# A first tile's norm split over two engines and two load queues, and a low-rank gate projection in four column groups of the array

## The chip, the cores and the metric

The kernel runs on all 8 cores of one Trainium2 chip (two dies, cores 0 to 3 and 4 to 7). Each core handles one prompt of 2048 tokens and four sample sequences of 8 tokens. The metric is the device time of the slowest core in microseconds. The kernel before took 2364.44 us (median of 3 runs, 2363.14 to 2366.65).

Some executions fall into a slower state, in which the cores of one die have a lower granted TensorE clock (in the trace of the kernel before, die 1 had 0.897 and 2576.0 us, die 0 had 0.993 and 2355.7 us).

- An *undisturbed die* is a die of one execution on which all four cores have a granted clock above 0.985.
- Each such die gives the mean of its four spans. I average these over all executions of a kernel and subtract the same average for the kernel before, run in the same series. The result is quoted with its standard error.

This measure is not the metric (in the fast runs of the kernel before the slowest core is 6 to 13 us above the mean of the cores). It uses more of the data and compares like with like.

## The reference, cut to what matters

```python
# D_MODEL 1024; GLA: 4 heads, DK 128, DV 256, gate rank 16
x = x + 0.5 * swiglu_ffn(rmsnorm(x, g[0]), w_in, w_out)       # first thing that any tile does: a norm of x
h = rmsnorm(x, g[1])
q, k, v, g_lr, r = split(h @ w_in)                            # g_lr has 16 columns
log_a = log_sigmoid(g_lr @ w_g2 + b_g) / 16                   # 16 -> 512: the second gate matrix
# for every chunk of the recurrence (the sample sequences have one chunk of 8 tokens):
o = attn @ v  +  (q * exp(cum)) @ state                       # inside the chunk + from the old state
# ... output norm, output gate, w_out; second half-FFN; shared K/V; a second layer with window attention
```

## The kernel before

Activations are transposed: 1024 features lie as 8 chunks of 128 partitions, with tokens along the free axis. Each core has four prompt tiles (t0 to t3, 512 tokens each) and one sample tile (32 tokens). Tiles are written as Python generators. A scheduler of the kernel's own runs them when the kernel is *built* and fixes the instruction order of every engine, from an estimated cost of each operation.

```python
def c_mm(count, n):                     # estimated cost of matmuls, us
    return count * max(n / 2400.0 + 0.0026, 0.0265)

# Threads.run: the operation that could start first by the estimates, ties within 0.15 us by urgency
cands = [(S.start_of(th[3][1], th[3][3], th[3][4]), th) for th in self.live if th[3] is not None]
...
m = min(c[0] for c in cands) + self.TIE
th = min((c for c in cands if c[0] <= m), key=lambda c: self.urgency(c[1]))[1]
```

The load of x and the squares of the norm. ScalarE (ACT) squares eight chunks, VectorE (DVE) adds them up one after the other, and one TensorE (PE) matmul with a matrix of ones sums the partitions.

```python
def load_x(T, prev):
    nq = 4 if T.n == 512 else 1
    for q in range(nq):
        ...
        yield O(SP, (lambda e, q=q, w=w, src=src, ms=ms: e.dma_start(out=..., in_=src[:, q * w:(q + 1) * w])), ...)
    for m in range(8):
        yield from square(T, m)           # ACT square into T.h[m]; DVE add to a running sum

def norm_stats(T):
    ...
    ms = [T.sum] if n == 512 else range(8)
    yield mm(PS[b][:, 0:n], [(ones, T.h[:, m, :]) for m in ms], ...)
    ...                                   # Ln and Exp on ACT; then DVE makes h = x * gain * rs
```

The gate of the recurrence: eight matmuls with a 128x16 stationary (the operand `lhsT`; the trace shows its load as an LDWEIGHTS of 90 ns beside each matmul), then per head one matmul with a 16x128 stationary.

```python
yield from mmh(T, (PS[b][0:16, :],), lambda kt, z: WLR[:, kt, :], ["WLR"], (b,), n)
...
yield copy(ACT, glr, PS[b][0:16, :], n, [("ps", b)], [gk])
...
yield mm(PS[b], [(WG2[0:16, hd * 128:(hd + 1) * 128], glr)], [gk, "WG2"], b, n)
```

The sample tile's recurrent output, four times (one sequence each). Two matmuls of 8 columns alternate, the first with 32 rows and the second with 128:

```python
for hd in range(4):
    for f in range(2):
        e.matmul(po[:, hd * 2 + f, :], lhsT=vv[...], rhs=am[:, hd, c8], start=True, stop=False)         # 32 rows
        ins = e.matmul(po[:, hd * 2 + f, :], lhsT=S0b[...], rhs=qT[:, hd, c8], start=False, stop=True)  # 128 rows
```

The softmax here doesn't subtract the row's maximum and nothing guards it: scores larger than these inputs give would overflow.

Of the kernel before, what the change touches and what calls it, by code (L numbers as in the profile page):

```python
# [227 lines left out]
def need(cond):  # L228
    return ("need", cond)
# [80 lines left out]
def build():  # L310
    nc = bass.Bass("TRN2", target_bir_lowering=False)

    def din(name, shape):
        return nc.dram_tensor(name, list(shape), F32, kind="ExternalInput").ap()
# [4 lines left out]
    xp = din("xp", [4, 128, 4096]); xs = din("xs", [128, 256]); st_in = din("st", [16, 128, 256])  # L319
    ck = din("ck", [4, 128, 3328]); cv = din("cv", [4, 128, 3328])  # L320
    wfi = din("wfi", [4 * NF, 128, 2048]); wfo = din("wfo", [32, 128, 2688])
    wgl = din("wgl", [16, 128, 2048]); wlr = din("wlr", [128, 128]); gg2 = din("gg2", [16, 512])
    wkv = din("wkv", [2, 128, 2048]); wqd = din("wqd", [3, 128, 2048]); wod = din("wod", [4, 128, 1536])
    cbd = din("cbd", [128, B_END - 128]); cfd = din("cfd", [128, A_END])
    rpd = din("rpd", [4, 2, 128, 512]); rsd = din("rsd", [128, 64])
# [10 lines left out]
    CB = A("CB", [128, B_END], BF16)  # L336
    CF = A("CF", [128, A_END], F32)
    SM = A("SM", [128, 8], F32)
    WLR = A("WLR", [128, 8, 16], BF16)
    WG2 = A("WG2", [16, 512], BF16)  # L340
    U = A("U", [128, 4, 256], F32)
    Sbf = A("Sbf", [128, 4, 256], BF16)
    KT = A("KT", [128, 2, 2048], BF16)
# [232 lines left out]
    def xk(T, m):  # L576
        return ("x", T.b, m)

    def hk(T, m):
        return ("h", T.b, m)  # L580

    def rk(T, what):
        return ("R", T.b, what)
# [56 lines left out]
# [3 lines that stand above are left out]
            ms = range(q * 8 // nq, (q + 1) * 8 // nq)  # L643
            if prev is not None:
                yield need(lambda: all(("y", prev.nm, m) in done for m in ms))
            if T.t == 1:
                after = units[(0, "fi0", 3 + 2 * q)]
                yield need(lambda: after.ready)
            w = len(ms) * T.n
            src = xp[T.t] if T.n == 512 else xs  # L650
            yield O(SP, (lambda e, q=q, w=w, src=src, ms=ms: e.dma_start(
                out=T.x[:, ms[0]:ms[-1] + 1, :].rearrange("p m n -> p (m n)"), in_=src[:, q * w:(q + 1) * w])),
                [after.key] if T.t == 1 else [], writes=[xk(T, m) for m in ms], cost=0.1, dma="x%s_%d" % (T.b, q), nbytes=w * 512)
        for m in range(8):
            yield from square(T, m)

# [22 lines left out]
    def norm_stats(T):  # L679

        n = T.n
        sqn = T.sqn
        yield need(lambda: all(("sq", T.nm, sqn, m) in done for m in range(8)))
        (b,) = yield from get_banks(1)
        ms = [T.sum] if n == 512 else range(8)
        yield mm(PS[b][:, 0:n], [(ones, T.h[:, m, :]) for m in ms], [hk(T, m) for m in ms] + ["ONE"], b, n)
        (i,) = yield from T.pool.get("rs", 1, 1)
        rs = T.pool.aps[i]
        k = T.pool.key(i)
        yield act(rs, PS[b][:, 0:n], AF.Ln, n, [("ps", b)], [k], bias=EPS)  # L690
        put(b)
        yield act(rs, rs, AF.Exp, n, [k], [k], scale=-0.5)
        T.sqn += 1
        return i
# [105 lines left out]
    def gla(T):  # L800
# [2 lines left out]
        h8 = hks(T)  # L803
        pool = T.pool
        (b,) = yield from get_banks(1)
        yield from mmh(T, (PS[b][0:16, :],), lambda kt, z: WLR[:, kt, :], ["WLR"], (b,), n)
        (gi,) = yield from pool.get("glr", 1, 1)
        glr, gk = pool.aps[gi][0:16, 0:256].bitcast(BF16), pool.key(gi)
        yield copy(ACT, glr, PS[b][0:16, :], n, [("ps", b)], [gk])
        put(b)  # L810
        gates = {}

        def gate():
            for hd in range(4):
                i, k_ = yield from pool.get("gate", 2, 6)
                a, c = pool.aps[i], pool.aps[k_]
                ka, kc = pool.key(i), pool.key(k_)
                (b,) = yield from get_banks(1)
                yield mm(PS[b], [(WG2[0:16, hd * 128:(hd + 1) * 128], glr)], [gk, "WG2"], b, n)
                yield act(a, PS[b], AF.Exp, n, [("ps", b), "negb"], [ka], scale=-1.0, bias=negb[:, hd:hd + 1])  # L820
                put(b)
                yield act(a, a, AF.Ln, n, [ka], [ka], bias=1.0)
                yield O(DVE, lambda e: e.tensor_tensor_scan(out=c, data0=CB[:, B_SC:B_SC + 512], data1=a, initial=0.0, op0=ALU.mult, op1=ALU.add),  # L823
                        [ka, "CB"], [kc], c_dve(1000))
                yield act(a, c, AF.Exp, n, [kc], [ka], scale=-1.0 / 16)
                yield act(c, c, AF.Exp, n, [kc], [kc], scale=1.0 / 16)
                yield copy(DVE, T.dec[:, hd, :], a[:, 127::128], 4, [ka], [("dec", T.b, hd)])
                gates[hd] = (i, k_)
            pool.put("glr", gi)
# [177 lines left out]
    def gla_s(T):  # L1007
# [19 lines left out]
        pk_ = [T.pool.key(i) for i in ids]  # L1027
        EQ, EK = A4, C4
        (b,) = yield from get_banks(1)
        yield from mmh(T, (PS[b][0:16, 0:n],), lambda kt, z: WLR[:, kt, :], ["WLR"], (b,), n)  # L1030
        glr = KB[0:16, 896:928]
        yield copy(ACT, glr, PS[b][0:16, 0:n], n, [("ps", b)], [gk])
        put(b)
# [57 lines left out]
        yield tt(am, pa, CB[0:32, B_MS:B_MS + 32].unsqueeze(1).to_broadcast([32, 4, 32]), ALU.mult, 128, [("ps", b), "CB"], [gk])  # L1091
        put(b)
        gv = [rk(T, ("gv", hd)) for hd in range(4)]
        for s in range(4):
            c8 = slice(s * 8, s * 8 + 8)
            us, ub = (yield from use(T, "S0", s)), (yield from use(T, "S0b", s))
            S0 = us.ap.bitcast(F32).rearrange("p (h w) -> p h w", h=4)
            S0b = ub.ap.rearrange("p (h w) -> p h w", h=4)
            yield copy(ACT, S0b, S0, 1024, [us.key], [ub.key])
            (b,) = yield from get_banks(1)  # L1100
            po = PS[b][:, 0:64].rearrange("p (m n) -> p m n", m=8)

            def fo(e, c8=c8, po=po, S0b=S0b):
                ins = None
                for hd in range(4):
                    for f in range(2):
                        e.matmul(po[:, hd * 2 + f, :], lhsT=vv[:, hd * 256 + f * 128:hd * 256 + (f + 1) * 128], rhs=am[:, hd, c8], start=True, stop=False)
                        ins = e.matmul(po[:, hd * 2 + f, :], lhsT=S0b[:, hd, f * 128:(f + 1) * 128], rhs=qT[:, hd, c8], start=False, stop=True)
                return ins
            yield O(PE, fo, [gk, ub.key] + gv, [("ps", b)], 1.68)  # L1110
            yield copy(ACT, oT[:, :, c8], po, 64, [("ps", b)], [rk(T, "go")])
            put(b)
            yield O(DVE, (lambda e, s=s: e.tensor_scalar(out=kms, in0=ktok, scalar1=CF[0:32, A_SQ + s:A_SQ + s + 1], scalar2=None, op0=ALU.mult)),
                    [gk, "CF"], [rk(T, "kms")], c_dve(512, 2))
            for hp in range(2):
                (b,) = yield from get_banks(1)
                pk = PS[b].rearrange("p (a w) -> p a w", a=2)

                def fk(e, hp=hp, pk=pk):
                    ins = None  # L1120
                    for a in range(2):
                        hd = 2 * hp + a
                        ins = e.matmul(pk[:, a, :], lhsT=kms[:, hd, :], rhs=vv[:, hd * 256:(hd + 1) * 256], start=True, stop=True)
                    return ins
                yield O(PE, fk, [rk(T, "kms")] + gv, [("ps", b)], c_mm(2, 256))
                for a in range(2):
                    hd = 2 * hp + a
                    yield stt(S0[:, hd, :], S0[:, hd, :], EQ[:, hd, s * 8 + 7:s * 8 + 8], pk[:, a, :], ALU.mult, ALU.add, 256, [("ps", b), us.key] + pk_, [us.key])
                put(b)
            yield O(SP, (lambda e, s=s, S0=S0: e.dma_start(out=sts_o[s * 4:(s + 1) * 4].rearrange("h p d -> p h d"), in_=S0)), [us.key], [],  # L1130
                    cost=0.1, dma="sts%d" % s, nbytes=524288)
            us.left -= 1
            ub.left -= 1
# [448 lines left out]
    def prologue():  # L1582

        yield need(lambda: units[(0, "fi0", 4)].ready)
        yield O(PL, lambda e: e.dma_start(out=CB[:, 128:], in_=cbd[:, :]), [], ["CB"], cost=1.0, dma="c1", nbytes=(B_END - 128) * 512)
        yield O(PL, lambda e: e.dma_start(out=WG2[:], in_=gg2[:, :]), [], ["WG2"], cost=1.0, dma="c2", nbytes=32768)
        yield O(PL, lambda e: e.dma_start(out=WLR[:].rearrange("p a b -> p (a b)"), in_=wlr[:, :]), [], ["WLR"], cost=1.0, dma="c3", nbytes=65536)
        yield O(SP, lambda e: e.dma_start(out=stabs[:], in_=rsd[:, :]), [], ["stabs"], cost=0.1, dma="c4", nbytes=32768)
        yield O(DVE, lambda e: e.tensor_scalar(out=negb, in0=G[:, 56:60], scalar1=-1.0, scalar2=None, op0=ALU.mult), ["CF"], ["negb"], 0.1)
        yield O(PL, lambda e: e.memset(U[:], 0.0), [], [("U", hd) for hd in range(4)], 2.0)  # L1590
# [17 lines left out]
def make_in_maps(inp, ncores=8):  # L1608
# [8 lines left out]
    def cols(w, k):  # L1617

        return w.reshape(k, 128, -1).transpose(1, 0, 2)
# [14 lines left out]
    for h in range(4):  # L1634
# [1 line left out]
    wgl = np.stack([w.reshape(128, 2048) for w in wg])  # L1636
    kvw, wq, wo = f(inp["kv_w"]), f(inp["attn_w_q"])[0], f(inp["attn_w_out"])[0]
    shared = {
        "wfi": f(wfi), "wfo": f(wfo), "wgl": f(wgl), "wlr": f(cols(glr, 8).reshape(128, 128)), "gg2": f(inp["gla_w_gate2"])[0],
        "wkv": f(np.stack([cols(kvw[:, i * 256:(i + 1) * 256], 8).reshape(128, 2048) for i in range(2)])),  # L1640
        "wqd": f(np.stack([cols(wq[:, i * 256:(i + 1) * 256], 8).reshape(128, 2048) for i in range(3)])),
        "wod": f(np.stack([cols(wo[:, i * 256:(i + 1) * 256], 6).reshape(128, 1536) for i in range(4)])),
# [40 lines left out]
```

## Time and profile before

| | kernel before |
|---|---|
| time, median of the first 3 runs | 2364.44 us |
| span and granted clock of core 0 in the trace | 2359.6 us, 0.993 |
| PE / DVE / ACT busy on core 0 | 98% / 52% / 50% |
| gate projection, second gate matrix, recurrent output (busy time on PE) | 8.6, 6.2, 11.4 us |

First look at the spans of the cores of the kernel before.

```profile
core 0: 2359.6 us, clock 0.993
...
core 2: 2362.8 us, clock 0.993
...
die 0 (median of its cores): 2355.7 us, clock 0.993
die 1 (median of its cores): 2576.0 us, clock 0.897
```

The page of core 0 of the kernel before: busy time by engine (PEld is TensorE's loading of weights), and the chain that ended last, by engine.

```profile
PE 2306.4 (98%) x14660; PEld 1129.2 (48%) x14660; DVE 1219.9 (52%) x2180; ACT 1172.5 (50%) x2316; POOL 317.2 (13%) x599
...
PE 94%; DMA 5%; issue 1%; ACT 0%; DVE 0%; SPq 0%; POOL 0%; POOLq 0%; ACTq 0%; DVEq 0%
```

TensorE is the bound. Work taken off it counts, unless it then waits for something else.

The groups of PE instructions that the change touches, kernel before, core 0. Columns: line, engine, operation, output and inputs, rows*columns of the stationary, shape, count, then busy time in us and the mean ns of one, then the idle time before them.

```profile
L615 PE MATMUL pst<-h,WLR 128*16 128x512 bf16 x32 | 8.6, 380 | 0.0
...
L615 PE MATMUL pst<-pb,WG 16*128 16x512 bf16 x16 | 6.2, 385 | 0.0
L1108 PE MATMUL pst<-KT,ring 128*128 128x8 bf16 x32 | 5.8, 180 | 0.0
L1107 PE MATMUL pst<-KT 32*128 32x8 bf16 x32 | 5.6, 175 | 0.0
```

The mean of one (380 ns and more) isn't what a matmul costs in a stream, where full-row matmuls of this shape start 216 ns apart (kernel before, core 0). For that cost one takes the distances of successive starts, in the timeline (start, length, engine, line, what, count). Kernel before, PE of core 0:

```profile
187.69 0.60 PE L615 MATMUL pst<-h,WLR 128*16 128x512 bf16 x2
188.22 1.90 PE L615 MATMUL pst<-h,ring 128*128 128x512 bf16 x8
190.06 0.38 PE L615 MATMUL pst<-pb,WG 16*128 16x512 bf16 x1
190.37 1.05 PE L615 MATMUL pst<-ring,h 128*128 128x256 bf16 x8
...
226.62 0.17 PE L1107 MATMUL pst<-KT 32*128 32x8 bf16 x1
226.72 0.18 PE L1108 MATMUL pst<-KT,ring 128*128 128x8 bf16 x1
...
228.30 0.38 PE L863 MATMUL pst<-CB,r 128*128 128x128 bf16 x4
```

From the second gate matrix's start to the next is 190.37 - 190.06 = 0.31 us, where a full-row matmul of 512 columns takes 0.216 from start to start. The recurrent-output block runs from 226.62 to 228.30, 1.68 us for 16 tiny matmuls.

The start of the kernel before, all engines of core 0. The last column is the idle time before, and what ended it:

```profile
1.97 2.73 SPq L651 DMA_DIRECT2D x<-xp  x4
...
9.98 1.15 ACT L620 ACTIVATE h<-x 128x512 bf16<-128x512 f32 x2 [2.87 <-DMA x<-xp]
...
17.45 0.69 DVE L628 TENSOR_TENSOR h<-pb,h 128x512 bf16<-128x512 f32 x1 [0.17 <-DVE pb L628]
...
21.06 2.08 DVE L631 SCALAR_TENSOR_TENSOR h<-x,CF,pb 128x512 bf16<-128x512 f32 x3 [0.73 <-ACT pb L620]
```

ACT gets the first quarter of x at about 10 us, the last DVE add starts at 17.45 and the first normed h at 21.06. Until then TensorE has almost nothing to do.

### The profile page before, as it was taken

Reading aid. Unit: us, or ns where it says so; the run is one execution under the profiler, and the core shown is the slowest. Engines: PE = TensorE matmul, PEld = TensorE weight load, DVE = VectorE, ACT = ScalarE, POOL = GpSimd, SP = SyncE. Lnnn points to the kernel's source line nnn. Section 1 sums busy time; section 2 is a strip of 40 time slices with the busy share of each in tenths; the row PEclk is TensorE's granted clock in tenths of the full one; section 3 lists DMA queues with packets and bytes.
Section 4 is the critical chain, followed back from the end, with each engine's and each line's share of the span. In section 5 each row is a group of like instructions: output and inputs, shape, how many; then the busy total and the mean of one; then the engine's idle time right before and its main releaser. Section 6 shows DMA issues by size and latency. Waiting matters only on the chain.

```text
span 2589.4 us, 42668 instructions; the slowest of 8 cores (2351.7 to 2589.4 us)
## 1 busy us (share of the span) xinstructions
PE 2542.9 (98%) x14660; PEld 1190.5 (46%) x14660; DVE 1223.3 (47%) x2180; ACT 1177.0 (45%) x2316; POOL 317.7 (12%) x599
## 2 busy tenths in 40 slices
PE   7999999999999999999999989999999999999999
PEld 3445444544444444455444435444544444444444
DVE  4424464445533446646543243454466335653742
ACT  5524544463443246455453124533555533753642
POOL 1111111101111111111111011011111111111110
PEclk8888888888888889999998878888999999999999
DMA  9986788778867788998897787667789989689794
GB/s 190 150 122 108 128 133 120 113 105 122 135 115 127 123 146 146 169 159 134 157 156 133 151 139 125 108 117 114 137 153 166 167 153 172 116 138 156 145 173 93
DMA packets 101362, 357.08 MB, mean 138 GB/s; under 512 B 12528, under 2 KB 17440, under 8 KB 101024
## 3 DMA queue, kind: packets, MB, share of 16 engines
q0 software_dynamic: 84032, 326.10, 77.7%
q1 hardware_dynamic: 17120, 28.25, 3.6%
q8 instruction: 122, 2.00, 0.3%
q14 instruction: 88, 0.72, 0.1%
HBM read 662.88 MB, written 15.40 MB: 262 GB/s over the span
## 4 chain that ended last, share of the span: by engine, by line
PE 96%; DMA 3%; issue 1%; ACT 0%; DVE 0%; SPq 0%; ACTq 0%; POOL 0%; POOLq 0%; DVEq 0%
PE pst L615 92%; DMA ring<-wfo 1%; DMA ring<-wfi 1%; PE pst L1410 1%; DMA ring<-ck 0%; PE pst L1349 0%; PE pst L987 0%; PE pst L970 0%; PE pst L988 0%; PE pst L1371 0%; DMA x<-xp 0%; PE pst L1433 0%; PE pst L1375 0%; PE pst L957 0%; PE pst L863 0%
## 5 line engine op out<-in xcount | busy, mean ns | idle before, releaser
L615 PE MATMUL pst<-h,ring 128*128 128x512 bf16 x6144 | 1531.1, 410 | 4.1 <-DVE h L631 3.3
L615 PEld LDWEIGHTS pst<-h,ring 128*128 128x128 bf16 x6144 | 623.5, 103 | 804.9 <-issue 471.8
L615 PE MATMUL pst<-r,ring 128*128 128x512 bf16 x3136 | 780.9, 409 | 6.4 <-DMA ring<-wfo 6.4
L620 ACT ACTIVATE pb<-pb 128x512 f32<-128x512 f32 x856 | 534.8, 629 | 64.7 <-DVE pb L823 4.4
L620 ACT ACTIVATE pb<-pst 128x512 f32<-128x512 f32 (+1 forms) x472 | 278.8, 595 | 567.6 <-PE pst L615 560.7
L628 DVE TENSOR_TENSOR pb<-pb,pst 128x512 f32<-128x512 f32 x368 | 252.2, 686 | 547.3 <-ACT pb L620 539.4
L615 PEld LDWEIGHTS pst<-r,ring 128*128 128x128 bf16 x3136 | 318.5, 103 | 415.6 <-issue 232.7
L511 POOL DMA_DIRECT2D ring<-wfi x336 | 178.0, 530 | 1224.4 <-PE pst L615 1150.7
L620 ACT ACTIVATE h<-x 128x512 bf16<-128x512 f32 x192 | 119.0, 627 | 391.3 <-DVE x L631 305.0
L628 DVE TENSOR_TENSOR r<-pb,pst 128x512 bf16<-128x512 f32 x336 | 230.6, 687 | 46.2 <-DVE pb L628 40.3
L631 DVE SCALAR_TENSOR_TENSOR x<-pst,x 128x512 f32<-128x512 f32 x128 | 88.3, 690 | 261.7 <-PE pst L615 261.4
L631 DVE SCALAR_TENSOR_TENSOR h<-x,CF,pb 128x512 bf16<-128x512 f32 x224 | 150.8, 746 | 13.4 <-ACT pb L620 12.6
L511 POOL DMA_DIRECT2D ring<-wfo x128 | 67.7, 529 | 605.5 <-PE pst L615 496.7
L628 DVE TENSOR_TENSOR pb<-pb,h 128x512 f32<-128x512 f32 x120 | 82.4, 689 | 43.7 <-ACT h L620 42.6
L615 PE MATMUL pst<-ring,h 128*128 128x256 bf16 x640 | 86.9, 302 | 0.0
L620 ACT ACTIVATE spb<-pst 128x32 f32<-128x32 f32 (+2 forms) x111 | 21.7, 198 | 125.0 <-PE pst L615 124.4
L615 PEld LDWEIGHTS pst<-ring,h 128*128 128x128 bf16 x640 | 67.4, 107 | 18.6 <-issue 5.1
L615 PEld LDWEIGHTS pst<-hsb,ring 128*128 128x128 bf16 x1536 | 53.9, 97 | 40.6 <-issue 35.4
L615 PE MATMUL pst<-hsb,ring 128*128 128x32 bf16 x1536 | 54.4, 178 | 14.1 <-DMA ring<-wfi 14.0
L511 POOL DMA_DIRECT2D ring<-wgl x64 | 33.9, 531 | 260.7 <-PE pst L615 238.9
L624 ACT COPY r<-pst 128x512 f32<-128x512 f32 (+3 forms) x104 | 51.0, 491 | 23.6 <-PE pst L1375 11.4
L628 DVE TENSOR_TENSOR x<-x,pst 128x512 f32<-128x512 f32 x64 | 43.9, 686 | 29.8 <-PE pst L615 29.7
(151 smaller groups left out, 1113.6 us busy)
## 6 DMA issues: line engine op xcount, KB each, us to landing
ring<-wfi POOLq DMA_DIRECT2D x336, 512.0 KB, 7.4
ring<-wfo POOLq DMA_DIRECT2D x128, 672.0 KB, 8.0
ring<-wgl POOLq DMA_DIRECT2D x64, 512.0 KB, 6.7
x<-xp SPq DMA_DIRECT2D x16, 512.0 KB, 9.6
y_p<-x SPq DMA_DIRECT2D x32, 256.0 KB, 7.8
ring<-wqd POOLq DMA_DIRECT2D x12, 512.0 KB, 9.7
ring<-wod POOLq DMA_DIRECT2D x16, 384.0 KB, 8.8
ring<-wkv POOLq DMA_DIRECT2D x8, 512.0 KB, 8.3
```

The source lines that it names most:

```text
L511: yield O(PL, (lambda e, u=u, dst=dst: e.dma_start(out=dst, in_=u.src)), first.get(u.uid, []), writes=[u.key], cost=1.0, dma="w%d_%d" % (s ...
L615: ins = e.matmul(out, lhsT=l, rhs=r, start=(start and i == 0), stop=(stop and i == last), skip_group_check=skip)
L620: return O(ACT, lambda e: e.activation(out=out, in_=in_, func=func, scale=scale, bias=bias), reads, writes, c_act(n))
L624: return O(ACT, lambda e: e.copy(out=out, in_=in_), reads, writes, c_act(n))
L628: return O(DVE, lambda e: e.tensor_tensor(out=out, in0=a, in1=b, op=op), reads, writes, c_dve(n, rate))
L631: return O(DVE, lambda e: e.scalar_tensor_tensor(out=out, in0=a, scalar=s, in1=b, op0=op0, op1=op1), reads, writes, c_dve(n))
L1410: ins = e.matmul(PS[bs[hp]][0:nk, rr * 64 + jj * 32:rr * 64 + jj * 32 + 32], lhsT=KT[hp * 64:hp * 64 + 64, jj, sl_(r, nk, 16)], rhs=T.QT[h ...
```

## The change

There are three parts, all meant to take time off TensorE or off the start:

1. *Start.* The first tile's squares are split between ACT and DVE, TensorE adds the eight of them with eight accumulating matmuls instead of DVE's chain of adds, and the odd quarters of x are issued from ACT's queue.
2. *Gate.* The eight gate-projection matmuls go to four groups of 32 columns of the array, which can run at once (in the trace before, the attention's 128*64 pairs start 3 to 4 ns apart). They leave four partial sums of two chunks each, on four groups of 32 partitions. The second gate matrix is stacked four times (padded to 32 rows each), so that its matmul, now with 128 rows, adds the partial sums.
3. *Recurrent output of the sample tile.* All 32-row matmuls are done in one run of 8 for the four sequences together, and the four blocks keep only their 128-row matmuls. DVE adds the two parts.

```diff
@@ load_x
-            yield O(SP, (lambda e, q=q, w=w, src=src, ms=ms: e.dma_start(
+            yield O(ACT if T.t == 0 and q % 2 else SP, (lambda e, q=q, w=w, src=src, ms=ms: e.dma_start(
...
+        if T.t == 0:
+            T.sum = None
+            for m in range(8):
+                if m % 2:
+                    yield stt(T.h[:, m, :], T.x[:, m, :], 1.0 / 1024, T.x[:, m, :], ALU.mult, ALU.mult, ...)
+                else:
+                    yield act(T.h[:, m, :], T.x[:, m, :], AF.Square, T.n, ..., scale=1.0 / 32)
+                done.add(("sq", T.nm, 0, m))
+            return
@@ norm_stats
-        ms = [T.sum] if n == 512 else range(8)
-        yield mm(PS[b][:, 0:n], [(ones, T.h[:, m, :]) for m in ms], [hk(T, m) for m in ms] + ["ONE"], b, n)
+        ms = [T.sum] if n == 512 and T.sum is not None else range(8)
+        for m in ms:
+            yield mm(PS[b][:, 0:n], [(ones, T.h[:, m, :])], [hk(T, m), "ONE"], b, n, start=(m == ms[0]), stop=(m == ms[-1]))
@@ gla
-        yield from mmh(T, (PS[b][0:16, :],), lambda kt, z: WLR[:, kt, :], ["WLR"], (b,), n)
+        hn = T.hn
+        for kt in range(8):
+            yield need(lambda: ("h", T.nm, hn, kt) in done)
+            p = slice(kt % 4 * 32, kt % 4 * 32 + 32)
+            yield O(PE, (lambda e: e.matmul(PS[b][p, :], lhsT=WLR[:, kt, :], rhs=T.h[:, kt, :], start=(kt < 4), stop=(kt >= 4))),
+                    [hk(T, kt), "WLR"], [("ps", b)], 0.06)
...
-                yield mm(PS[b], [(WG2[0:16, hd * 128:(hd + 1) * 128], glr)], [gk, "WG2"], b, n)
+                yield mm(PS[b], [(WG2[:, hd * 128:(hd + 1) * 128], glr)], [gk, "WG2"], b, n)
@@ gla_s
+        def fi(e):
+            ins = None
+            for m in range(8):
+                ins = e.matmul(PS[b][:, m * n:(m + 1) * n], lhsT=vv[:, m * 128:(m + 1) * 128], rhs=am[:, m // 2, :], start=True, stop=True)
+            return ins
+        yield O(PE, fi, [gk] + gv, [("ps", b)], c_mm(8, n))
...
-                        e.matmul(po[:, hd * 2 + f, :], lhsT=vv[...], rhs=am[:, hd, c8], start=True, stop=False)
-                        ins = e.matmul(po[:, hd * 2 + f, :], lhsT=S0b[...], rhs=qT[:, hd, c8], start=False, stop=True)
+                        ins = e.matmul(po[:, hd * 2 + f, :], lhsT=S0b[...], rhs=qT[:, hd, c8], start=True, stop=True)
...
-            yield copy(ACT, oT[:, :, c8], po, 64, [("ps", b)], [rk(T, "go")])
+            yield tt(oT[:, :, c8], oT[:, :, c8], po, ALU.add, 64, [("ps", b), rk(T, "go")], [rk(T, "go")])
... (cut: the padded and stacked gate weights, 0.29 MB more to load by the kernel's own byte counts)
```

More of the change, by code (lines that the diff above doesn't have):

```diff
@@ L321, in build @@
     wfi = din("wfi", [4 * NF, 128, 2048]); wfo = din("wfo", [32, 128, 2688])
-    wgl = din("wgl", [16, 128, 2048]); wlr = din("wlr", [128, 128]); gg2 = din("gg2", [16, 512])
+    wgl = din("wgl", [16, 128, 2048]); wlr = din("wlr", [128, 256]); gg2 = din("gg2", [128, 512])
     wkv = din("wkv", [2, 128, 2048]); wqd = din("wqd", [3, 128, 2048]); wod = din("wod", [4, 128, 1536])
@@ L338, in build @@
     SM = A("SM", [128, 8], F32)
-    WLR = A("WLR", [128, 8, 16], BF16)
-    WG2 = A("WG2", [16, 512], BF16)
+    WLR = A("WLR", [128, 8, 32], BF16)
+    WG2 = A("WG2", [128, 512], BF16)
     U = A("U", [128, 4, 256], F32)
@@ L650, in load_x @@
             src = xp[T.t] if T.n == 512 else xs
-            yield O(SP, (lambda e, q=q, w=w, src=src, ms=ms: e.dma_start(
+            yield O(ACT if T.t == 0 and q % 2 else SP, (lambda e, q=q, w=w, src=src, ms=ms: e.dma_start(
                 out=T.x[:, ms[0]:ms[-1] + 1, :].rearrange("p m n -> p (m n)"), in_=src[:, q * w:(q + 1) * w])),
                 [after.key] if T.t == 1 else [], writes=[xk(T, m) for m in ms], cost=0.1, dma="x%s_%d" % (T.b, q), nbytes=w * 512)
+        if T.t == 0:
+            T.sum = None
+            for m in range(8):
+                if m % 2:
+                    yield stt(T.h[:, m, :], T.x[:, m, :], 1.0 / 1024, T.x[:, m, :], ALU.mult, ALU.mult, T.n, [xk(T, m)], [hk(T, m)])
+                else:
+                    yield act(T.h[:, m, :], T.x[:, m, :], AF.Square, T.n, [xk(T, m)], [hk(T, m)], scale=1.0 / 32)
+                done.add(("sq", T.nm, 0, m))
+            return
         for m in range(8):
@@ L805, in gla @@
         (b,) = yield from get_banks(1)
-        yield from mmh(T, (PS[b][0:16, :],), lambda kt, z: WLR[:, kt, :], ["WLR"], (b,), n)
+        hn = T.hn
[4 more added lines that the diff above has]
+                    [hk(T, kt), "WLR"], [("ps", b)], 0.06)
         (gi,) = yield from pool.get("glr", 1, 1)
-        glr, gk = pool.aps[gi][0:16, 0:256].bitcast(BF16), pool.key(gi)
-        yield copy(ACT, glr, PS[b][0:16, :], n, [("ps", b)], [gk])
+        glr, gk = pool.aps[gi][:, 0:256].bitcast(BF16), pool.key(gi)
+        yield copy(ACT, glr, PS[b], n, [("ps", b)], [gk])
         put(b)
@@ L1029, in gla_s @@
         (b,) = yield from get_banks(1)
-        yield from mmh(T, (PS[b][0:16, 0:n],), lambda kt, z: WLR[:, kt, :], ["WLR"], (b,), n)
+        yield from mmh(T, (PS[b][0:16, 0:n],), lambda kt, z: WLR[:, kt, 0:16], ["WLR"], (b,), n)
         glr = KB[0:16, 896:928]
@@ L1093, in gla_s @@
         gv = [rk(T, ("gv", hd)) for hd in range(4)]
+        (b,) = yield from get_banks(1)
+        def fi(e):
[4 more added lines that the diff above has]
+        yield O(PE, fi, [gk] + gv, [("ps", b)], c_mm(8, n))
+        yield copy(ACT, oT.rearrange("p m n -> p (m n)"), PS[b][:, 0:8 * n], 8 * n, [("ps", b)], [rk(T, "go")])
+        put(b)
         for s in range(4):
@@ L1106, in fo @@
                     for f in range(2):
-                        e.matmul(po[:, hd * 2 + f, :], lhsT=vv[:, hd * 256 + f * 128:hd * 256 + (f + 1) * 128], rhs=am[:, hd, c8], start=True, stop=False)
-                        ins = e.matmul(po[:, hd * 2 + f, :], lhsT=S0b[:, hd, f * 128:(f + 1) * 128], rhs=qT[:, hd, c8], start=False, stop=True)
-                return ins
-            yield O(PE, fo, [gk, ub.key] + gv, [("ps", b)], 1.68)
-            yield copy(ACT, oT[:, :, c8], po, 64, [("ps", b)], [rk(T, "go")])
+                        ins = e.matmul(po[:, hd * 2 + f, :], lhsT=S0b[:, hd, f * 128:(f + 1) * 128], rhs=qT[:, hd, c8], start=True, stop=True)
+                return ins
+            yield O(PE, fo, [gk, ub.key], [("ps", b)], 0.3)
+            yield tt(oT[:, :, c8], oT[:, :, c8], po, ALU.add, 64, [("ps", b), rk(T, "go")], [rk(T, "go")])
             put(b)
@@ L1585, in prologue @@
         yield O(PL, lambda e: e.dma_start(out=CB[:, 128:], in_=cbd[:, :]), [], ["CB"], cost=1.0, dma="c1", nbytes=(B_END - 128) * 512)
-        yield O(PL, lambda e: e.dma_start(out=WG2[:], in_=gg2[:, :]), [], ["WG2"], cost=1.0, dma="c2", nbytes=32768)
-        yield O(PL, lambda e: e.dma_start(out=WLR[:].rearrange("p a b -> p (a b)"), in_=wlr[:, :]), [], ["WLR"], cost=1.0, dma="c3", nbytes=65536)
+        yield O(PL, lambda e: e.dma_start(out=WG2[:], in_=gg2[:, :]), [], ["WG2"], cost=1.0, dma="c2", nbytes=262144)
+        yield O(PL, lambda e: e.dma_start(out=WLR[:].rearrange("p a b -> p (a b)"), in_=wlr[:, :]), [], ["WLR"], cost=1.0, dma="c3", nbytes=131072)
         yield O(SP, lambda e: e.dma_start(out=stabs[:], in_=rsd[:, :]), [], ["stabs"], cost=0.1, dma="c4", nbytes=32768)
@@ L1638, in make_in_maps @@
     shared = {
-        "wfi": f(wfi), "wfo": f(wfo), "wgl": f(wgl), "wlr": f(cols(glr, 8).reshape(128, 128)), "gg2": f(inp["gla_w_gate2"])[0],
+        "wfi": f(wfi), "wfo": f(wfo), "wgl": f(wgl), "wlr": f(np.pad(cols(glr, 8), ((0, 0), (0, 0), (0, 16))).reshape(128, 256)),
+        "gg2": f(np.tile(np.pad(f(inp["gla_w_gate2"])[0], ((0, 16), (0, 0))), (4, 1))),
         "wkv": f(np.stack([cols(kvw[:, i * 256:(i + 1) * 256], 8).reshape(128, 2048) for i in range(2)])),
```

## The prediction

> **What bounds the kernel.** TensorE. The recorded run is in the slow state (one die at clock 0.897), so I read cores 0 and 2 of the undisturbed die (2359.6 and 2362.8 us, clock 0.993). The page of core 0 has PE busy 98%, DVE 52%, ACT 50%; its chain is 94% PE, 5% DMA. Successive starts in the trace are 216 ns apart for a 128x512 matmul, 25 ns for 128x32; start gaps over 0.4 us beyond that pace add up to only 37 to 52 us per core. From 20 to 150 us the DMA share is about 1.03: there both are full.
>
> **Costs, from the trace (core 0).**
> 1. Gate projection, four prompt tiles: 32 matmuls with a 128*16 stationary, 216 ns apart, one by one. In four column groups neighbours run at once: the attention's 128*64 pairs already start 3 to 4 ns apart. By the changed kernel's instruction order the 32 fall into 11 runs and 12 rounds: 20 x 216 ns = 4.3 us go. The runs' switch costs stay.
> 2. Second gate matrix, 16 matmuls with 16 rows: each costs about 93 ns extra going in (309 to 312 where 216 is normal) and 100 going out (317). [...] With 128 rows there is no switch: 16 x 0.19 = 3.1 us.
> 3. Sample tile's recurrent output: 64 matmuls of 8 columns alternate between 32 and 128 rows, 108 and 112 ns apart: 4 blocks of 1.68 us. After: 32 full-row ones at about 25 ns and one run of 8 with 32 rows (0.4 us with its switches): 1.2 us. Saves 5.5 us. The added copy and adds are off the path.
> Sum on TensorE: 12.9 us, in stages (170 to 420, 1380 to 1600 us) where it does not wait for DMA.
> 4. Start. On core 2 the last quarter of x lands at 13.7, the DVE adds end at 15.9, the sum matmul starts at 17.0, h comes from 19.4. The change should bring h about 3 us earlier; 7 extra matmuls fall into idle time. But the first weight units land at 16.5 and 20.5, DMA is at 100%, and TensorE already waits for weights at 44 to 48 us on three of four cores. An earlier start is mostly paid back there[...]. The second queue: [...] issuing four quarters took 1.9 to 2.7 us here. The first quarter, which releases the first weights, may even land later. Net: -1 us (-3 to +1).
>
> **Sum.** -13 us of TensorE time, some 80% passing through (weight waits near 540 to 600, 850 and the 8 to 10 us one at 1330 us may grow), and -1: 2364.4 - 11.5 = 2353 us. Eight times in ten between 2344 and 2362. Faster by over 2%: 0.01; within 2%: 0.98; slower: 0.01.
>
> **What would show it.** Gate projection matmuls 3 to 5 ns apart within a round; second-gate matmuls at 216 ns without jumps; recurrent-output blocks of about 0.2 us; first h before 17 us, but the first weight matmul not before 17 and more waiting for weights before 50 us; the wait near 1320 still there.
>
> **What would make it wrong.** The instruction order changes throughout the first 450 us and may add or remove waits. Four column groups might not overlap. A DMA-bound first stage could swallow the later gains, or a gain at the start could pass through whole.

80% of -13 us, and -1 for the start, come to about -11.5 us. The -1 was given as one figure, without parts, so it is my estimate. In the traces of core 0 the loads of WG and WLR grew by 144 KB together (16 to 128 and 32 to 64 KB); at the 177 GB/s that this core moved from 20 to 150 us before, that is an estimated 0.8 us.

## More of the kernel before

The verdicts on whole runs use fast runs alone.

At 82 us the sum matmul of the second prompt tile's norm (`h,CB`, CB holds the ones) stands in the timeline of the kernel before, core 0:

```profile
81.99 0.38 PE L615 MATMUL pst<-h,CB 128*128 128x512 bf16 x1
...
82.20 0.56 PE L615 MATMUL pst<-hsb,ring 128*128 128x32 bf16 x16
...
82.61 3.61 PE L615 MATMUL pst<-h,ring 128*128 128x512 bf16 x16
...
84.58 5.39 DVE L631 SCALAR_TENSOR_TENSOR h<-x,CF,pb 128x512 bf16<-128x512 f32 x8
```

While ACT and DVE turn that sum into the tile's normed h (from 84.58), TensorE has 16 matmuls of the sample tile (`hsb`) and 16 of another prompt tile to do. It does not wait. The same kernel does wait at the same kind of place later: at about 935 us TensorE stands idle for 2.9 us on all four undisturbed cores, between a norm's sum and its h.

## The result, and the profile after

The changed kernel is correct and took 2357.65 us (median of 4 runs, 2355.72 to 2358.66), beside 2363.79 us for the kernel before in the same rounds (4 runs, 2361.63 to 2366.65). That is 6.1 us less. The ratio is 0.9972, with a 95% interval of 0.9955 to 0.999. Ratios are the mean time of one kernel's fast runs over that of the other's fast runs of the same rounds, so they are not quite the ratio of the medians quoted. The time lies inside the predicted range; of the predicted gain of 11.5 us about half arrived.

The kernel after, spans of the cores. Both dies are undisturbed:

```profile
core 0: 2342.4 us, clock 0.994
core 1: 2355.6 us, clock 0.993
...
die 0 (median of its cores): 2350.4 us, clock 0.993
die 1 (median of its cores): 2349.3 us, clock 0.993
```

The same page lines of core 0 after the change:

```profile
PE 2295.2 (98%) x14643; PEld 1125.0 (48%) x14643; DVE 1218.0 (52%) x2181; ACT 1168.3 (50%) x2309; POOL 317.0 (14%) x599
...
PE 95%; DMA 3%; issue 1%; ACT 1%; DVE 0%; SPq 0%; ACTq 0%; DVEq 0%; POOLq 0%
```

PE's busy time fell by 11.2 us. (Core 0 alone fell by 17 us in span, but cores of one run differ by that much: 2338.7 to 2355.6 after. One core of one run proves nothing at this size.)

The groups that the change made, kernel after, core 0:

```profile
L615 PE MATMUL pst<-pb,WG 128*128 128x512 bf16 x16 | 6.1, 379 | 0.0
...
L822 PE MATMUL pst<-h,WLR 128*32 128x512 bf16 x32 | 5.2, 388 | 0.0
...
L1134 PE MATMUL pst<-KT,ring 128*128 128x8 bf16 x32 | 1.4, 166 | 0.0
...
L1116 PE MATMUL pst<-KT 32*128 32x32 bf16 x8 | 0.4, 173 | 0.0
```

And their timeline on PE, kernel after:

```profile
182.91 0.40 PE L822 MATMUL pst<-h,WLR 128*32 128x512 bf16 x3
...
222.73 0.34 PE L1134 MATMUL pst<-KT,ring 128*128 128x8 bf16 x8
222.93 2.32 PE L615 MATMUL pst<-h,ring 128*128 128x512 bf16 x10
```

Three gate-projection matmuls together take 0.40 us, as long as one (0.38 us for the single one at 183.23): in a run of eight, starts within a group of four were 2 to 4 ns apart, with one step of 217 ns between the two groups. A recurrent-output block takes 222.93 - 222.73 = 0.20 us, where it took 1.68. The second gate matrix now goes at the 216 ns of its neighbours. All three TensorE savings are there. So the missing microseconds are somewhere else.

The start, kernel after, core 0:

```profile
1.07 0.88 ACTq L651 DMA_DIRECT2D x<-xp  x2
...
1.97 1.21 SPq L651 DMA_DIRECT2D x<-xp  x2
...
11.77 0.63 ACT L620 ACTIVATE h<-x 128x512 bf16<-128x512 f32 x1 [0.19 <-DMA x<-xp]
...
19.09 2.08 DVE L631 SCALAR_TENSOR_TENSOR h<-x,CF,pb 128x512 bf16<-128x512 f32 x3 [2.84 <-ACT spb L620]
```

The issue of x is done sooner, but the first quarter *lands* later. Over the undisturbed cores, the first square of the prompt tile starts before at 8.3 us (mean; core 0 is late with 9.98) and after at 11.6; the last square starts at 13.8 and 15.8 (after the change DVE does 1.39 us of the sample tile's work first); the first DMA of weights, which waits for the first quarter, is issued at 8.8 and 12.1. The first four weight DMAs wait for one quarter each. On two queues they go out back to back, some 0.55 us apart, from 12.29 us on core 0: none of the later three still has to wait. By the landing records of this core the two odd quarters, issued first (1.07 and 1.51), landed at 6.66 and 10.60 us, then the first quarter at 11.69 and the third at 12.92; on all 8 cores the first quarter landed after both odd ones. In the one-queue kernel of experiment 9 the weight DMAs go out at 8.54, 10.80, 12.13 and 14.56, as one quarter after the other lands. Meanwhile the DMA engines of core 0 run short of work after the change: their share is 0.58 and 0.37 from 10 to 12 and 12 to 14 us, where it was 1.01 and 0.80. The split squares win that back and a little more: the first normed h comes at 20.2 before and 19.3 after, 0.9 us earlier instead of the 3 that I had written.

And a new hole, at the place shown above. Kernel after, core 0, same place:

```profile
80.41 0.38 PE L615 MATMUL pst<-h,CB 128*128 128x512 bf16 x1
...
82.55 5.38 DVE L631 SCALAR_TENSOR_TENSOR h<-x,CF,pb 128x512 bf16<-128x512 f32 x8
...
83.56 2.23 PE L615 MATMUL pst<-h,ring 128*128 128x512 bf16 x6 [2.76 <-DVE h L631]
...
86.05 4.66 PE L615 MATMUL pst<-h,ring 128*128 128x512 bf16 x16
```

The scheduler now puts the second tile's first projection right behind its own norm's sum, and TensorE waits 2.76 us for DVE. Then 16 matmuls take 4.66 us instead of 3.61. The windows of the same core say why. Columns: stretch, its length, then busy us of PE, PEld, DVE, ACT, POOL, then PEclk (the granted clock), DMA share and GB/s.

```profile
82.00:86.00 4.00, 2.38 (x21) 0.97 (x22) 4.00 (x7) 0.21 (x1) 0.53 (x1) 0.85 1.08 206
86.00:90.00 4.00, 4.00 (x22) 1.68 (x19) 2.22 (x5) 1.49 (x5) 0.53 (x1) 0.73 1.05 156
```

The granted clock is 0.85 and 0.73 in those two stretches; in the kernel before it is 1.00 in both. In finer windows it is exactly 0.50 from about 84.8 to 88.2 us, some 3.4 us. There the starts of 512-column matmuls are 427 ns apart instead of 216. The idle time that went before it was 2.76 us. The clock lost is 4 x 0.15 + 4 x 0.27 = 1.7 us. Hole and half clock together are about 4.5 us on this core. The hole is on all 8 cores and in 5 of 8 the half clock follows (on the other three it costs 2.8 us alone). So the two suspects are the start itself and the order.

### The profile page after: what moved, and what is told of

It reads as the page before. It is cut to its first block, busy times and chain, and to the rows that moved or that the text cites. A ratio compares the mean times of both kernels' runs of the same rounds, so it can differ in the third digit from the quotient of the medians.

```text
span 2355.6 us, 42703 instructions; the slowest of 8 cores (2338.7 to 2355.6 us)
## 1 busy us (share of the span) xinstructions
PE 2298.3 (98%) x14643; PEld 1124.9 (48%) x14643; DVE 1218.2 (52%) x2181; ACT 1169.9 (50%) x2309; POOL 317.0 (13%) x599
## 4 chain that ended last, share of the span: by engine, by line
PE 93%; DMA 5%; issue 1%; ACT 0%; DVE 0%; SPq 0%; DVEq 0%; POOLq 0%; ACTq 0%; POOL 0%
PE pst L615 89%; DMA ring<-wfi 2%; DMA ring<-wfo 2%; PE pst L1436 1%; PE pst L1375 1%; DMA x<-xp 0%; DMA ring<-ck 0%; PE pst L1397 0%; PE pst L987 0%; PE pst L1004 0%; PE pst L1005 0%; ACT pb L620 0%; PE pst L1401 0%; PE pst L1459 0%; PE pst L974 0%
## 5 line engine op out<-in xcount | busy, mean ns | idle before, releaser
L615 PE MATMUL pst<-h,ring 128*128 128x512 bf16 x6144 | 1387.6, 381 | 9.4 <-DVE h L631 6.9
L615 PEld LDWEIGHTS pst<-h,ring 128*128 128x128 bf16 x6144 | 589.8, 98 | 707.4 <-issue 37.2
L615 PE MATMUL pst<-r,ring 128*128 128x512 bf16 x3136 | 707.2, 380 | 7.4 <-DMA ring<-wfo 7.4
L620 ACT ACTIVATE pb<-pb 128x512 f32<-128x512 f32 x856 | 535.4, 630 | 71.6 <-DVE pb L840 12.1
L615 PEld LDWEIGHTS pst<-r,ring 128*128 128x128 bf16 x3136 | 302.1, 98 | 364.6 <-issue 12.8
L631 DVE SCALAR_TENSOR_TENSOR x<-pst,x 128x512 f32<-128x512 f32 x128 | 88.2, 689 | 216.4 <-PE pst L615 215.7
L615 PE MATMUL pst<-ring,h 128*128 128x256 bf16 x640 | 74.4, 273 | 0.0
L615 PEld LDWEIGHTS pst<-hsb,ring 128*128 128x128 bf16 x1536 | 52.4, 96 | 32.2 <-issue 13.8
L615 PEld LDWEIGHTS pst<-ring,h 128*128 128x128 bf16 x640 | 62.3, 98 | 11.2
L620 ACT ACTIVATE h<-pst 128x512 bf16<-128x512 f32 (+4 forms) x96 | 46.4, 510 | 18.3 <-PE pst L1375 10.3
```

The source lines that it names most:

```text
L615: ins = e.matmul(out, lhsT=l, rhs=r, start=(start and i == 0), stop=(stop and i == last), skip_group_check=skip)
L620: return O(ACT, lambda e: e.activation(out=out, in_=in_, func=func, scale=scale, bias=bias), reads, writes, c_act(n))
L631: return O(DVE, lambda e: e.scalar_tensor_tensor(out=out, in0=a, scalar=s, in1=b, op0=op0, op1=op1), reads, writes, c_dve(n))
```

## The experiments

All kernels below gave correct results, and each was run with five timed rounds. "-x" is x us faster than the kernel before, on undisturbed dies, with the standard error. The first four kernels shared one chip, on which one die was slow in every run of the kernel before, so that they have no ratio of fast runs. The next eight ran in two series on another chip and have both measures.

### 1. The TensorE parts without the start

Edit: the changed kernel with the whole first part undone.

```diff
 load_x / norm_stats: as in the kernel before
 gla, gla_s, gate weights: as in the changed kernel
```

> The kernel before with the gate projection, the second gate matrix and the sample tile's recurrent output of the change, but with the old start (one queue, squares on ACT with DVE adds). Theory 1 (the start gives time back: its new instruction order leaves a hole of 2.9 us at the second tile's first norm and the early stage waits more on weights, while the 12.9 us of TensorE work pass through): 11 to 13 us below the kernel before, ratio about 0.995, so 5 us below the whole change; no hole near 85 us. Theory 2 (the TensorE savings themselves are half lost to later waits for weights, the start is neutral): about 6 us below before, the same as the whole change.

Measured: -11.1 ± 1.2 us (6 dies against 9), and no hole at 80 us. In the last series I ran the same kernel again:

> The version with the old start once more, as the control on this chip: 11 to 12 us below before.

Measured: -11.1 ± 0.6; ratio of fast runs 0.9968 (0.9951 to 0.9984). The two agree. My sum for these parts was 12.9 us of TensorE time; 86% of it arrives, where I had guessed 80%. So the TensorE terms are right, and what is missing in the whole change is lost by its start.

### 2. The start alone

Edit: the kernel before with only the first part of the diff (split squares, sum on TensorE, two queues).

```diff
 load_x / norm_stats: as in the changed kernel
 gla, gla_s, gate weights: as in the kernel before
```

> The kernel before with the new start alone (two queues, split squares, sum on TensorE). Theory 1: 3 to 6 us slower than before, ratio about 1.002, with the 2.9 us hole near 85 us in the trace. Theory 2: within 1 us of before.

Measured: +9.4 ± 1.1 us (7 dies). The start alone makes the kernel slower. The trace has the hole (2.77 us before the projection on core 0) and half clock after it in all four undisturbed cores (granted clock 0.64 from 86 to 90 us on core 0). The size is more than the whole change lost. About half of it is the hole with its half clock. The mean granted clock of these dies was 0.9912 instead of 0.9929: by that, an estimated 0.0017 x 2360 = 4.0 us of clock were lost, of which 1.7 belong to the hole, so half-clock stretches elsewhere may be another 2.3 us. The rest, about 2.6 us, I cannot name. It shows that such parts do not simply add up, because each gives another instruction order.

### 3. The second queue taken away

Edit to the changed kernel:

```diff
-            yield O(ACT if T.t == 0 and q % 2 else SP, (lambda e, ...: e.dma_start(
+            yield O(SP, (lambda e, ...: e.dma_start(
```

> The whole change, but all four quarters of the first x on the SP queue. If the second queue is what costs (it makes the first quarter land at 11 us instead of 7 to 10, and so the first weights go out later): first quarter lands 2 to 4 us earlier and the time is 2 to 3 us below the whole change. Theory 1 with the hole as cause: within 1 us of the whole change, hole near 85 us still there. Theory 2: the same.

Measured: -7.3 ± 1.3 us (7 dies). On the undisturbed die of its trace the first square came at 7.8 us and the first h at 16.3 (means of four cores), 3 us earlier than in the changed kernel (19.3). Yet the time is that of the changed kernel (its control below: -8.0 ± 0.9). The hole of 2.8 us is still there on all cores, with half clock after it on one of the four undisturbed ones. So the queue does what I suspected to the start, but taking it away gained nothing measurable in this order (0.7 ± 1.6 us slower, and over two chips).

### 4. The second tile's first projection held back

Edit to the changed kernel, to take the hole away by order:

```diff
             if j == 0 and n == 512:
+                if T.t == 1 and f == 0:
+                    yield need(lambda: ("h", T.nm, T.hn, 5) in done)
                 yield from mmh(T, (g, up), ...)
```

> The whole change with the second tile's first projection held back in the instruction order until most of its normed chunks have been placed, so TensorE has the first tile's and the sample tile's matmuls to do in between. Theory 1: the hole near 85 us goes and the time is 2 to 3 us below the whole change (2355 us). Theory 2 (early holes are paid back anyway because weights set the pace there): within 1 us of the whole change.

Measured: -6.8 ± 1.3 us (6 dies), a miss. The hole did not close; it changed its cause. The held kernel, PE of core 0:

```profile
82.93 0.38 PE L615 MATMUL pst<-h,CB 128*128 128x512 bf16 x1
85.69 0.58 PE L615 MATMUL pst<-hsb,ring 128*128 128x32 bf16 x16 [2.38 <-DMA ring<-wfi]
86.10 5.15 PE L615 MATMUL pst<-h,ring 128*128 128x512 bf16 x15
```

What stands there instead now is work whose weights have not arrived: TensorE waits for `ring<-wfi`, 2.38 us here and up to 4.1 on other cores, and the half clock follows on all four undisturbed cores (granted clock 0.59 from 86 to 90 us on core 0). This neither supports nor refutes that the order costs the time, as the hole was not removed.

### 5. The changed kernel again, as a control

> The whole change once more, unaltered, as the control for the runs of this chip. 6 to 8 us below before on the cores of an undisturbed die.

Measured: -8.0 ± 0.9 us (8 dies); ratio 0.9968 (0.9952 to 0.9984). The hole is on all cores, the half clock on 7 of 8. With -11.1 for the TensorE parts alone, the start costs 3.1 us inside the whole change.

### 6. An order near the old one, on one and on two queues

The last of the eight sum matmuls gets an estimated cost of 3.2 us instead of 0.22 in the scheduler's model. No instruction changes; only the order does. The value was chosen by building kernels and reading their instruction order.

```diff
-            yield mm(PS[b][:, 0:n], [(ones, T.h[:, m, :])], ...)
+            o = mm(PS[b][:, 0:n], [(ones, T.h[:, m, :])], ...)
+            yield o if not (n == 512 and len(ms) == 8 and m == 7) else o[:5] + (3.2,) + o[6:]
```

On one queue:

> The change on one queue, where the cost that the scheduler's own model gives to the last sum matmul is raised, so that the instruction order comes out nearly as in the version with the old start (25 of some 1440 rows differ, against 190). The hardware work is that of the one-queue version. Theory 1a (order is what costs): 2 to 4 us below the one-queue version, no hole near 80 us, and if an earlier start is worth anything also below the version with the old start, that is 13 to 15 us below before. Theory 1b (weights set the pace in the first 150 us, so an earlier start is worth nothing): the first weight matmul 3 to 4 us earlier than with the old start, but the second tile's projection units after 100 us at the same times, and the same total as the version with the old start within 1.5 us (11 us below before).

Measured: -10.8 ± 0.8 us (10 dies); ratio 0.9957 (0.9944 to 0.9969). The hole is 0.4 us at most and there is no half clock from 74 to 100 us. But this order lets the sample tile's second weight unit go ahead of the prompt's first, so that the first weight matmuls of the prompt start at 21.3 us, no sooner than before. It tells the order's effect, not that of an earlier start.

On two queues, the same edit:

> The same instruction order, with the second queue back. If the second queue delays the start: the first quarter of x lands at 10 to 11 us and the first weight matmul starts 3 to 4 us later than in the run with the same order and one queue. By theory 1b the total is the same within 1.5 us all the same; if the start counts, 2 to 4 us more.

Measured: -9.4 ± 0.8 us (13 dies); ratio 0.9962 (0.9948 to 0.9976). The second queue costs 1.4 ± 1.1 here, by the difference of the two: the right sign, not more. This run says something about the order too. It has the changed kernel's work and queues, no hole and no half clock from 74 to 96 us on any core, and yet it is only 1.5 ± 1.2 us below the control of the same series (experiment 5). On the other side, TensorE waits longer for weights in it: 7.6 us from 15 to 52 us, where the control has 3.1 (means of 8 cores). Taking the hole away is not worth its full size when the new order adds waits elsewhere.

### 7. The gate parts alone, and the recurrent output alone

> The kernel before with the gate projection in four column groups and the 128-row second gate matrix alone. By the sum of prediction 4.3 + 3.1 = 7.4 us of TensorE time; passing through at the rate that the version with both showed (11 of 12.9): 6 us below before. If the 0.29 MB of additional gate weights cost in the full early stage: only 4 to 5 us.

Measured: -7.2 ± 0.6 us (11 dies); ratio 0.9968 (0.9955 to 0.998). Predicted for TensorE: 4.3 + 3.1 = 7.4.

> The kernel before with the sample tile's recurrent output alone. TensorE work 5.5 us less; if it passes through as the gate part did (6 to 7 of 7.4 us): 4.5 to 5.5 us below before. If it is lost to waits for weights around 310 to 350 us and 540 to 600 us: 0 to 2 us.

Measured: -4.3 ± 0.7 us (12 dies); ratio 0.9993 (0.9979 to 1.0007), so the fast runs alone do not show it. Predicted for TensorE: 5.5. The two add up to 11.5, and together they gave 11.1.

### 8. Order alone

The same kind of edit with a cost of 0.6 instead of 3.2, everything else as in the changed kernel, both queues too. It was picked because its built order has other work behind the second tile's sum and the first units in their old order.

```diff
+            yield o if not (n == 512 and len(ms) == 8 and m == 7) else o[:5] + (0.6,) + o[6:]
```

> The whole change, both queues, with another instruction order: the scheduler's model cost of the last of the eight sum matmuls is set from 0.22 to 0.6 us, nothing else. The order of the second tile's first norm then comes out as in the kernel before (first-tile work between the norm's sum and its use). The traces so far show the hole of 2.9 us near 85 us followed by an interval of 3.4 us at half clock in three of four cores. Theory (order, hole and half clock): no hole over 1 us and no half-clock interval between 70 and 100 us, and the total 2 to 4 us below the whole change, at 10 to 12 us below before. Rival (the start stage is paced by weights, order does not matter): same as the whole change, 8 to 9 us below before.

Measured: -11.8 ± 0.8 us (11 dies); ratio 0.996 (0.9947 to 0.9973), fast median 2356.19 beside 2365.77. The same place in this kernel, core 0:

```profile
80.94 0.38 PE L615 MATMUL pst<-h,CB 128*128 128x512 bf16 x1
...
81.16 0.56 PE L615 MATMUL pst<-hsb,ring 128*128 128x32 bf16 x16
...
81.56 3.61 PE L615 MATMUL pst<-h,ring 128*128 128x512 bf16 x16
...
83.09 5.38 DVE L631 SCALAR_TENSOR_TENSOR h<-x,CF,pb 128x512 bf16<-128x512 f32 x8
```

Other work stands in the gap again, 16 matmuls take 3.61 us, and the granted clock is 1.00. The order alone is worth 11.8 - 8.0 = 3.8 us (standard error 1.2, and over two series). The hole with its half clock is 2.8 to 4.5 us per core, and the waits for weights from 15 to 52 us are alike (3.3 us here, 3.1 in the control), so it can account for it. That it alone does is not shown: in the two traces the sequence of TensorE's groups differs at some 30 places (core 1), and with the hole two smaller waits go as well (see Open).

### 9. This order, on one queue

Edits 3 and 8 together: split squares, sum on TensorE, x from one queue, cost 0.6.

> The same instruction order with all four quarters of x on one queue, so that the first prompt matmul with weights starts near 17 us instead of 20 to 22. If an earlier start passes through: 2 to 4 us below the same order with two queues, 13 to 16 us below before. If weights pace the first 150 us: within 1 us of the same order with two queues, and of the version with the old start.

Measured: -14.6 ± 0.6 us (11 dies); ratio 0.9951 (0.9938 to 0.9964), fast median 2353.60 us beside 2365.77 for the kernel before. Its start, core 0:

```profile
1.96 2.26 SPq L651 DMA_DIRECT2D x<-xp  x4
...
8.01 0.63 ACT L620 ACTIVATE h<-x 128x512 bf16<-128x512 f32 x1 [0.72 <-DMA x<-xp]
...
17.50 2.08 DVE L631 SCALAR_TENSOR_TENSOR h<-x,CF,pb 128x512 bf16<-128x512 f32 x3 [2.68 <-ACT pb L620]
```

With one queue the first quarter is there at 8.0 us on core 0, and at 7.4 in the mean of 8 cores, instead of 12.1 in the kernel of experiment 8. TensorE's groups come in the same sequence in the two but for one place (core 1). The second queue costs 14.6 - 11.8 = 2.8 us (standard error 1.0; in the same series, same instruction costs). Against the old start with the same TensorE parts (-11.1 ± 0.6, same series) the split squares bring 3.5 us (standard error 0.8).

This version has the lowest time of all that were run. It is faster than the changed kernel by the undisturbed dies (-14.6 ± 0.6 against -8.0 ± 0.9, each beside the kernel before of its own series). The intervals of the two ratios of fast runs overlap a little, and the two did not run in one series.

## Why the prediction was right or wrong

The total was inside the range. The sum, term by term:

| term | predicted, us | measured, us |
|---|---|---|
| gate projection and second gate matrix | -7.4 of TensorE time | -7.2 ± 0.6 |
| recurrent output | -5.5 of TensorE time | -4.3 ± 0.7 |
| together, after 80% passing through | -10.3 | -11.1 ± 0.6 |
| start, net | -1 (-3 to +1) | +3.1 ± 1.1 (-8.0 against -11.1) |
| whole | -11.5 | -6.1 (medians), -8.0 ± 0.9 (dies, second series) |

**Right: "What bounds the kernel. TensorE."** Three savings counted from distances of starts in the trace arrived to 86%. The "distance of starts" was the right measure: by the busy column the second gate matrix goes from 6.2 to only 6.1 us.

**Right: the mechanism of the second queue.** I wrote that "The first quarter, which releases the first weights, may even land later." It landed 3 to 4 us later. That the odd quarters, issued first, keep it back fits the landing records after the change: on core 0 they landed at 6.66 and 10.60 us and the first quarter at 11.69, where on one queue before it landed first, at 9.89. The order of issue was not changed apart from the queue. In the trace the issue was short before (2.73 us for four quarters), and the runs show a cost of the second queue: 2.8 ± 1.0 us of the kernel's time in the order of experiments 8 and 9, 1.4 ± 1.1 in that of experiment 6, and none that could be measured in that of the changed kernel (experiment 3).

**Wrong in size: the start, "Net: -1 us (-3 to +1)".** This is the term of the sum that failed; it measured +3.1. Three terms make it up, by the experiments: the split squares on one queue in a good order -3.5, the second queue +2.8, the order +3.8. They are three steps along one chain of kernels, so their sum is 3.1 by construction, and by experiments 3 and 6 the sizes of the last two depend on the order in which they are measured. The first two together are -0.7, near my -1, but partly by luck, because:

- **Wrong: "An earlier start is mostly paid back there"**, at the weight waits before 50 us. With one queue and a good order, 2.8 to 3.5 us pass to the end. Those waits did not swallow it: from 24 to 52 us TensorE waits 2.1 us for weights in the early version, 2.0 in the same order on two queues and 2.5 with the old start and the same TensorE parts (means of 8 cores). The early version has its first weight matmul of the prompt at 17.8 us (mean of 8 cores), the kernel before at 21.3.
- **Not in the sum: the order.** "The instruction order changes throughout the first 450 us and may add or remove waits" stood only among what could go wrong. I knew of it and gave it a size of zero. It was worth 3.8 us by experiment 8, the largest of the three if only by a little, and 1.5 us by experiment 6.

**What would show it.** The gate, second-gate and recurrent-output signs all appeared with their numbers. "First h before 17 us" did not appear in the whole change (19.3), and appeared with one queue (means of 16.3 in the third experiment and 16.7 in the ninth). "More waiting for weights before 50 us" appeared in the traces, 1.6 us from 24 to 52 us after the change and 0.45 before, but it is no mark of an early start, as the old start with the same TensorE parts has 2.5. The wait near 1320 us on `wfo` was still there, 7.7 us on core 0 of the changed kernel, 10.1 before.

**Open.** Why the start alone cost 9.4 us is explained by the hole only to about half, and by the estimate of all lost clock to some 6.8 us. New waits of 0.9 and 1.4 to 1.6 us at about 270 and 285 us in the changed kernel were not tested separately; in the kernel of experiment 8 they are gone and a wait of 1.1 us at about 260 us stands there, so some 1.2 us of the order's 3.8 may be theirs. That half clock belongs to the cost of the hole was seen beside it, and not changed apart from it.

## What to carry to other kernels

When a build-time scheduler orders the instructions, a local change can also change the order far behind it, in ways that nobody chose (here 3.8 us of 2360, experiment 8): look at what stands behind each norm's sum (or any round trip over other engines) in the new order, and try the change in several orders before judging it. For an early load, put the piece that is needed first at the head of one queue; a second queue can make it later (here its first square started at 11.8 us instead of 8.0, core 0). Cost TensorE savings by distances of starts, not by busy time (from the second gate matrix's start to the next it was 316 to 318 ns before and mostly 216 after, core 0; the busy time went only from 6.2 to 6.1 us).

## What these traces showed of the hardware

- Granted clock after a wait: a stretch of 3.41 us at 0.50 followed the wait of 2.76 to 2.77 us on 5 of 8 cores in the trace of the changed kernel, the same hole on 7 of 8 in its second run (experiment 5), and a wait of 2.92 to 2.93 us at about 935 us on all four undisturbed cores of the kernel before. What sets the other cores apart was not shown.
- Granted clock of whole runs: in the fast run of the changed kernel, with TensorE busy 97 to 98% on all 8 cores, it is 0.991 to 0.995. On core 6 of the slow die in the trace before it is 0.81 at 300, 600, 900, 1500 and 1800 us and 1.00 at 1200, 2000 and 2200 us (stretches of 10 us), so this core moved between the two within one run. In the experiments a die was undisturbed in 121 of 144 cases on one chip and in 35 of 86 on the other.
- Full-array matmuls of 512 columns: in the kernel before, core 0, 98% of successive starts are 214 to 219 ns apart, and 0.5% are 420 to 436 ns apart, all of these from 22 to 27 us or in stretches at 0.50.
- Change of shape, in the kernel before, core 0: from a full-array matmul of 512 columns to the next start it was 311 to 312 ns instead of 216 when the next had 16 rows (second gate matrix) or 32 (recurrent output), so 95 to 96 ns more, and 309 ns when it had 16 columns (gate projection). From the second gate matrix to the next start it was 316 to 318, about 100 more. Small matmuls that alternate between 32 and 128 rows started 106 to 113 ns apart; the 128-row ones alone, in the kernel after, 25 to 28 ns.
- Two queues for one load: the first square of the first quarter started at 11.8 us in the changed kernel, instead of 8.0 on one queue (experiment 9, core 0), and the second queue cost the kernel up to 2.8 us, depending on the order.
